# Making the low halves of the first feed-forward weights with an accumulating DMA instead of a VectorE subtraction

## The chip, the cores and the metric

The program runs on one core of one Trainium2 chip. The metric is the device time of one execution in microseconds, the median of several runs. The engines are named as the profile names them: PE is TensorE (PEld its weight loads), DVE is VectorE, ACT is ScalarE, POOL is GpSimd and SP is SyncE, which here only issues DMAs.

## What is computed

Two transformer layers on a sequence of 512 positions of width 1024, and a final norm. Each layer has a projection, two groups of attention heads and an output projection, and after that a feed-forward part with 4096 hidden units and a squared ReLU:

```python
        x = x + jnp.einsum('bse,ed->bsd', mixed, w_o[l])

        h = rmsnorm(x, mlp_norm[l])
        u = jnp.square(jax.nn.relu(jnp.einsum('bsd,df->bsf', h, w_ff1[l])))
        x = x + jnp.einsum('bsf,fd->bsd', u, w_ff2[l])
    return rmsnorm(x, final_norm)
```

All of it is float32. The change touches only how the weights `w_ff1` of the first quarter of the hidden units are made ready for PE.

## The kernel before

**Products in three parts.** PE multiplies operands of the type fp32r. To keep float32 accuracy, every operand is split into a high part, its value rounded to fp32r, and a low part, the rest that the rounding left. A product is then three matmuls (function `three`, L298 to L302): high by high (L300), high weight by low activation (L301), low weight by high activation (L302). So each weight tile `raw` of 128 x 1024 floats gets a pair `whi` and `wlo`: `whi` is a rounding copy on ACT (L117), `wlo` is `raw - whi`, a subtraction on DVE (L133).

**Units and their order.** The weights are cut into units of 128 x 1024 floats that are used in a fixed order (`_unit_list`). In each layer come the projections, then eight units of the output projection (kind "o"), then the feed-forward part in four groups. Group 0 has eight units of kind "1": unit ("1", l, f) holds the 1024 x 128 block of `w_ff1` for 128 hidden units. In the order they are the units 32 to 39 of layer 0 and 170 to 177 of layer 1, and the instruction order below shows them with these numbers (`raw32`, `whi32`, `wlo32`). The groups 1 to 3 work otherwise (seven combined forms per quarter) and are not touched. After the eight units of group 0 come the units of `w_ff2` (kind "f", tiles named `q`).

**One unit on PE.** `block` takes a unit and makes, for eight slices of 128 input dimensions, three matmuls each of 128 x 128 by 128 x 512, 24 in all, into one bank named `f`. The low part of the weights is needed by the third matmul of the block. After the block `evict_whole` on ACT and DVE makes ReLU, square and their splits.

**When a unit is split.** `next` is called when PE's work on unit i is written, and calls `do_split` for the units ahead: two ahead while there is one pool of split tiles (two pairs), four ahead once the feed-forward part has added a second pool (`W.pools.append(f2)`), as far as the pair that a unit takes belongs to no unit still to be used. So unit 32 is split while the output projection still runs, into the pair of unit 30; unit 33 takes the pair of unit 31; units 34 and 36 take the two pairs of the new pool; units 35 and 39 take the pair of unit 32, unit 38 that of unit 33 and unit 37 that of unit 34. A program that lays out the instructions then sets each engine's order by priorities; the order on each engine is fixed before the run.

**Loads.** `raw` tiles stand in a ring of three. SP loads them (L110); a load waits until the tile three units before it has been read. POOL issues the DMAs that add to what stands in a tile (`accum_op=ALU.add`), at L879, L886 and L911: they make sums of weight blocks for the later groups. POOL's instructions run in their written order, so a DMA there waits for the one ahead of it to be issued.

Of the kernel before, what the change touches and what calls it, by code (L numbers as in the profile page):

```python
# [12 lines left out]
AF = mybir.ActivationFunctionType  # L13
ALU = mybir.AluOpType
# [37 lines left out]
def _unit_list():  # L52
    units = []
    def qk(l, cq, ck, b):
        units.append(("p", l, cq + b * P))
        units.append(("p", l, ck + b * P))

    for l in range(L):
        for item in ORDER:
            b = int(item[1])  # L60
            if item[0] == "d":
                units.append(("x", l, b, 0))
                units.append(("x", l, b, 1))
            elif item[0] == "s":
                qk(l, SBQ, SBK, b)
            elif item[0] == "w":
                units.extend(("w", l, part) for part in range(4))
            else:
                units.extend(("v", l, SBV + b * P, half) for half in range(2))
        for half in (1, 0):  # L70
            for j in range(4):
                units.append(("o", l, half, j))
        for g in range(GROUPS):
            if g == 0:
                units.extend(("1", l, f) for f in range(2 * GP))
            else:
                units.extend(("s", l, g, j, form) for j in range(2) for form in FORMS)
            for form in FORMS2:
                for c in range(GP // 2):
                    units.append(("f", l, g, form, c))  # L80
    return units


_UNITS = _unit_list()
# [4 lines left out]
_SLOT = {u: n for n, u in enumerate(_RING)}  # L89
# [4 lines left out]
class _Weights:  # L94
# [24 lines left out]
    def split_part(self, i, a, b):  # L119
        nc = self.nc  # L120
        if i not in self.tiles and i in self.home:
            self.tiles[i] = self.home[i]
        if i not in self.tiles:
            k = self.spot(i)
            self.owner[k] = i
            self.turn = k + 1
            hi = self.pools[k // 2].tile([P, 1024], F32R, tag="whi", name=f"whi{i}")
            lo = self.pools[k // 2].tile([P, 1024], F32R, tag="wlo", name=f"wlo{i}")
            self.tiles[i] = (hi, lo)
        hi, lo = self.tiles[i]  # L130
        raw = self.first if (i, b) == (0, P) else self.raw[i]
        h = self.round(hi[:, a:b], raw[:, a:b])
        self.last = h, nc.vector.tensor_tensor(  # L133
            out=lo[:, a:b], in0=raw[:, a:b], in1=hi[:, a:b].bitcast(F32), op=ALU.subtract)

# [1244 lines left out]
```

## Time and profile before

| what | value |
|---|---|
| median of three runs | 1123.38 us (1123.38 to 1124.75) |
| the profiled execution, its own time | 1124.32 us |
| its span from the first to the last instruction | 1122.5 us |
| first feed-forward group in the span, layer 0 | 238.6 to 282.7 us |
| the same in layer 1 | 793.9 to 841.6 us |

The profile is of one execution. Its span lies 1.8 us below that execution's own time, and that execution is 0.94 us above the median of the three runs. Rows of a timeline give start, duration, engine, line, operation, output and inputs, and in brackets how long the engine was idle before and what released it. The tiles' numbers are left out there: `whi<-raw` is any unit's rounding. Since ACT's order is fixed, the eight roundings `whi<-raw` of a layer's group 0 are the last eight before the first `whi<-q`.

### The profile page before, as it was taken

The numbers are of one execution on the slowest core, as the hardware profiler recorded it, in microseconds if no ns is written. First come the engines' busy times: TensorE is split into PE (matmuls) and PEld (weight loads), VectorE is DVE, ScalarE is ACT, GpSimd is POOL, SyncE is SP. The second block draws the span as 40 slices with busy tenths as digits, with TensorE's granted clock in tenths as the row PEclk, the third lists the DMA queues.
The fourth block names the chain that finished last, engine by engine and source line by source line (L and its number), as shares of the span: only waits on it lengthen the run. The fifth ranks groups of instructions, "written<-read, shape, count | busy, mean of one in ns | idle before, by whom it ended". The sixth has DMA issues, their size and how long they took to land.

```text
span 1122.5 us, 17199 instructions
## 1 busy us (share of the span) xinstructions
PE 1114.8 (99%) x6377; PEld 977.4 (87%) x6377; DVE 903.5 (80%) x1309; ACT 683.3 (61%) x1107; POOL 154.3 (14%) x233
## 2 busy tenths in 40 slices
PE   9999999999999999999999999999999999999997
PEld 6889889888899899899878898988888998998986
DVE  7788788798668778779877887887787788797787
ACT  6446666667558458467344566665774584674665
POOL 1001343101011001001000014430010010010011
PEclk9999999999999999999999999999999999999999
DMA  7466343269688678658324654612577877687462
GB/s 243 143 190 186 110 131 117 69 222 230 173 214 182 175 200 186 189 132 210 110 75 146 198 146 131 166 60 76 206 174 185 205 177 185 183 187 206 114 132 94
DMA packets 61043, 181.25 MB, mean 161 GB/s; under 512 B 7456, under 2 KB 8736, under 8 KB 60960
## 3 DMA queue, kind: packets, MB, share of 16 engines
q1 hardware_dynamic: 50160, 141.84, 40.1%
q0 software_dynamic: 10368, 37.75, 19.1%
q8 instruction: 50, 0.82, 0.3%
q10 hardware_dynamic: 432, 0.56, 0.1%
q14 instruction: 33, 0.27, 0.1%
HBM read 150.77 MB, written 4.19 MB: 138 GB/s over the span
## 4 chain that ended last, share of the span: by engine, by line
PE 98%; DVE 1%; DMA 0%; ACT 0%; issue 0%; POOL 0%; SPq 0%; POOLq 0%; DVEq 0%
PE X L300 9%; PE X L302 9%; PE X L301 9%; PE V L300 4%; PE V L301 4%; PE V L302 4%; PE wo L300 3%; PE wo L302 3%; PE wo L301 3%; PE f L302 3%; PE f L300 3%; PE f L301 3%; PE Y L301 2%; PE Y L302 2%; PE Y L300 2%; PE W L302 1%
## 5 line engine op out<-in xcount | busy, mean ns | idle before, releaser
L117 ACT ACTIVATE whi<-q 128x1024 fp32r<-128x1024 f32 x96 | 101.6, 1059 | 108.5 <-PE X L302 38.1
L133 DVE TENSOR_TENSOR wlo<-q,whi 128x1024 fp32r<-128x1024 f32 x96 | 117.2, 1222 | 46.4 <-ACT whi L117 46.2
L133 DVE TENSOR_TENSOR wlo<-raw,whi 128x1024 fp32r<-128x1024 f32 (+1 forms) x82 | 97.2, 1192 | 11.1 <-ACT whi L117 11.0
L117 ACT ACTIVATE whi<-raw 128x1024 fp32r<-128x1024 f32 (+1 forms) x82 | 80.9, 993 | 38.3 <-issue 8.9
L300 PE MATMUL X<-whi,Ah 128*128 128x512 f32 x248 | 97.6, 393 | 0.0
L301 PE MATMUL X<-wlo,Ah 128*128 128x512 f32 x248 | 96.7, 390 | 0.0
L302 PE MATMUL X<-whi,Al 128*128 128x512 f32 x248 | 96.7, 390 | 0.0
L133 DVE TENSOR_TENSOR wlo<-waves,whi 128x1024 fp32r<-128x1024 f32 x40 | 48.9, 1222 | 16.5 <-ACT whi L117 16.4
L117 ACT ACTIVATE whi<-waves 128x1024 fp32r<-128x1024 f32 x40 | 42.2, 1055 | 29.7 <-PE X L302 20.5
L300 PEld LDWEIGHTS X<-whi,Ah 128*128 128x128 f32 x248 | 46.6, 188 | 12.0 <-DVE y L1104 1.9
L302 PEld LDWEIGHTS X<-whi,Al 128*128 128x128 f32 x248 | 46.5, 188 | 9.8
L301 PEld LDWEIGHTS X<-wlo,Ah 128*128 128x128 f32 x248 | 46.6, 188 | 9.0
L302 PE MATMUL X<-h_hi,wlo 128*128 128x256 f32 x192 | 54.3, 283 | 0.0
L300 PE MATMUL X<-hxh,whi 128*128 128x256 f32 x192 | 54.3, 283 | 0.0
L301 PE MATMUL X<-hxl,whi 128*128 128x256 f32 x192 | 54.3, 283 | 0.0
L302 PE MATMUL X<-hxh,wlo 128*128 128x256 f32 x192 | 54.3, 283 | 0.0
L301 PE MATMUL X<-h_lo,whi 128*128 128x256 f32 x192 | 54.3, 283 | 0.0
L300 PE MATMUL X<-h_hi,whi 128*128 128x256 f32 x192 | 54.3, 283 | 0.0
L300 PE MATMUL f<-h_hi,whi 128*128 128x512 f32 x128 | 50.4, 394 | 0.0
L302 PE MATMUL f<-h_hi,wlo 128*128 128x512 f32 x128 | 49.9, 390 | 0.0
L301 PE MATMUL f<-h_lo,whi 128*128 128x512 f32 x128 | 49.8, 389 | 0.0
L240 DVE TENSOR_TENSOR Al<-x,Ah 128x512 fp32r<-128x512 f32 (+1 forms) x60 | 46.6, 793 | 3.8 <-ACT Ah L239 3.5
(712 smaller groups left out, 3701.6 us busy)
## 6 DMA issues: line engine op xcount, KB each, us to landing
raw<-in_w SPq DMA_DIRECT2D x78, 512.0 KB, 3.6
q<-in_w SPq DMA_DIRECT2D x48, 512.0 KB, 4.5
q<-in_w POOLq DMA_DIRECT2D x48, 512.0 KB, 7.5
waves<-in_w SPq DMA_DIRECT2D x28, 512.0 KB, 4.4
first_a<-in_w SPq DMA_DIRECT2D x12, 512.0 KB, 4.9
first_b<-in_w SPq DMA_DIRECT2D x12, 512.0 KB, 5.1
first_c<-in_w SPq DMA_DIRECT2D x12, 512.0 KB, 4.2
first_b<-in_w POOLq DMA_DIRECT2D x12, 512.0 KB, 6.8
```

The lines of the kernel that those rows point to most:

```text
L117: return self.nc.scalar.activation(o, src, AF.Copy)
L133: self.last = h, nc.vector.tensor_tensor(out=lo[:, a:b], in0=raw[:, a:b], in1=hi[:, a:b].bitcast(F32), op=ALU.subtract)
L240: nc.vector.tensor_tensor(out=lo, in0=src, in1=hi.bitcast(F32), op=ALU.subtract)
L300: nc.tensor.matmul(pt, ah, bh, start=first, stop=False, skip_group_check=goes_on),
L301: nc.tensor.matmul(pt, ah, bl, start=False, stop=False, skip_group_check=goes_on),
L302: nc.tensor.matmul(pt, al, bh, start=False, stop=last, skip_group_check=goes_on))
```

## The change

For units of kind "1", `wlo` is no longer made by DVE. ACT first writes the negative rounding into `wlo` (a copy with the scale -1, new L134), and then POOL issues a DMA (new L135) that adds the weights themselves from DRAM onto it: `wlo = -round(raw) + raw`. All other units still go through the subtraction. Lines of the changed kernel behind this place are four higher than in the kernel before.

```diff
         hi, lo = self.tiles[i]
         raw = self.first if (i, b) == (0, P) else self.raw[i]
         h = self.round(hi[:, a:b], raw[:, a:b])
+        if _UNITS[i][0] == "1":
+            nc.scalar.activation(lo[:, a:b], raw[:, a:b], AF.Copy, scale=-1.0)
+            self.last = h, nc.gpsimd.dma_start(lo[:, a:b], self.dram[_SLOT[i]][:, a:b], accum_op=ALU.add)
+            return
         self.last = h, nc.vector.tensor_tensor(
             out=lo[:, a:b], in0=raw[:, a:b], in1=hi[:, a:b].bitcast(F32), op=ALU.subtract)
```

The order of ACT at the end of layer 0's output projection, before the change (`h_hi` and `sq` are the splits and squares of the residual stream after each of its output blocks, L1005 begins the combined forms for the later groups):

```order
L259 ACTIVATE sq_2649<-x_71 128x512
L117 ACTIVATE whi32_2671<-raw32_2587 128x1024
L250 ACTIVATE h_hi_72<-x_71,begin_70 128x512
L259 ACTIVATE sq_2668<-x_71 128x512
L250 ACTIVATE h_hi_72<-x_71,begin_70 128x512
L259 ACTIVATE sq_2693<-x_71 128x512
L117 ACTIVATE whi33_2755<-raw33_2631 128x1024
L250 ACTIVATE h_hi_72<-x_71,begin_70 128x512
L259 ACTIVATE sq_2712<-x_71 128x512
L1005 ACTIVATE x_71<-x_71,begin_70 128x256 x4
L117 ACTIVATE whi34_2761<-raw34_2675 128x1024
```

The same place in the changed kernel:

```order
L263 ACTIVATE sq_2649<-x_71 128x512
L117 ACTIVATE whi32_2671<-raw32_2587 128x1024
L134 ACTIVATE wlo32_2672<-raw32_2587 128x1024
L254 ACTIVATE h_hi_72<-x_71,begin_70 128x512
L263 ACTIVATE sq_2668<-x_71 128x512
L254 ACTIVATE h_hi_72<-x_71,begin_70 128x512
L263 ACTIVATE sq_2694<-x_71 128x512
L117 ACTIVATE whi33_2756<-raw33_2631 128x1024
L134 ACTIVATE wlo33_2757<-raw33_2631 128x1024
L254 ACTIVATE h_hi_72<-x_71,begin_70 128x512
L263 ACTIVATE sq_2713<-x_71 128x512
L1009 ACTIVATE x_71<-x_71,begin_70 128x256 x3
```

The roundings stand where they stood, and each negated copy stands right behind its rounding.

POOL's order at the start of group 0 of layer 0, before the change (the last attention product, then the accumulating DMAs for the groups behind):

```order
L567 TENSOR_TENSOR sig0s313_2439<-sig0s313_2439,C0s313_2440 128x512
L879 DMA q10_0_2734<-in_w2 128x1024
L879 DMA q11_0_2735<-in_w2 128x1024
L911 DMA first_b0_2910<-in_w1 128x1024
L886 DMA q00_0_2732<-in_w2 128x1024
```

And in the changed kernel:

```order
L571 TENSOR_TENSOR sig0s313_2439<-sig0s313_2439,C0s313_2440 128x512
L135 DMA wlo32_2672<-in_w 128x1024
L135 DMA wlo33_2757<-in_w 128x1024
L135 DMA wlo34_2764<-in_w 128x1024
L135 DMA wlo35_2851<-in_w 128x1024
L135 DMA wlo36_2858<-in_w 128x1024
L883 DMA q10_0_2735<-in_w2 128x1024
L883 DMA q11_0_2736<-in_w2 128x1024
L135 DMA wlo37_2904<-in_w 128x1024
L135 DMA wlo38_2913<-in_w 128x1024
L915 DMA first_b0_2917<-in_w1 128x1024
L135 DMA wlo39_2968<-in_w 128x1024
```

Five of the eight new DMAs stand ahead of `q10` and `q11`, two behind them, and the last behind `first_b0`.

ACT's order further on in the changed kernel, at the third block's eviction (`norms<-f` is that eviction, the `Ah` rows are splits of the activations):

```order
L117 ACTIVATE whi38_2912<-raw38_2862 128x1024
L978 ACTIVATE norms_74<-f0_0_2_2849 128x512
L117 ACTIVATE whi37_2903<-raw37_2855 128x1024
L248 ACTIVATE Ah0_0_2738<-waves_75 128x256
L243 ACTIVATE Ah0_0_2738<-waves_75 128x256
L979 ACTIVATE norms_74<-norms_74 128x512
L134 ACTIVATE wlo37_2904<-raw37_2855 128x1024
L243 ACTIVATE Ah0_0_2738<-norms_74 128x256
L134 ACTIVATE wlo38_2913<-raw38_2862 128x1024
```

Here the negated copies do not follow their roundings directly: three small rows stand between those of unit 37.

## The prediction

> **What bounds the kernel now.** I read the page's first and fourth part first: who is busy, and which engine the chain that ended last runs over.
>
> ```profile
> PE 1114.8 (99%) x6377; PEld 977.4 (87%) x6377; DVE 903.5 (80%) x1309; ACT 683.3 (61%) x1107; POOL 154.3 (14%) x233
> PE 98%; DVE 1%; DMA 0%; ACT 0%; issue 0%; POOL 0%; SPq 0%; POOLq 0%; DVEq 0%
> ```
>
> PE is busy for 99% of the span and holds 98% of the chain. So nothing that DVE gives up can shorten the program unless PE waits for DVE somewhere, and everything that makes PE wait lengthens it by that wait. The PE column of the table of windows shows whether PE waits in the stage of the change (its columns: window and length, busy time of PE, PEld, DVE, ACT and POOL, granted clock, DMA share, GB/s).
>
> ```profile
> 238.00:244.00 6.00, 6.00 (x28) 4.99 (x27) 5.21 (x9) 5.17 (x10) 0.00 (x0) 1.00 0.53 181
> 244.00:250.00 6.00, 6.00 (x30) 4.94 (x29) 6.00 (x12) 4.13 (x6) 0.00 (x0) 1.00 0.91 321
> 794.00:800.00 6.00, 6.00 (x28) 4.99 (x27) 4.35 (x6) 4.25 (x6) 0.00 (x0) 1.00 0.32 103
> 800.00:806.00 6.00, 6.00 (x32) 4.95 (x32) 4.98 (x8) 3.80 (x7) 0.00 (x0) 1.00 0.91 309
> 244.00:262.00 18.00, 18.00 (x83) 14.89 (x82) 18.00 (x36) 13.26 (x20) 1.98 (x2) 1.00 0.89 304
> ```
>
> PE is busy without a gap at the start of group 0 in both layers. DVE is full from 244 to 262 us, and PE does not feel it. The list of PEld's waits by releaser, for the whole span, begins with this row (total, times, longest):
>
> ```profile
> PEld X L300 <- DVE y L1104: 1.9, 5, 0.4
> ```
>
> The longest entry that names DVE is 1.9 us, and it belongs to the chains `X`, behind group 0's blocks. So the most that a lighter DVE could give in this program is of that size, and in the stage of the change it is zero.
>
> **What goes and what comes.** The page's groups price the two instructions:
>
> ```profile
> L117 ACT ACTIVATE whi<-raw 128x1024 fp32r<-128x1024 f32 (+1 forms) x82 | 80.9, 993 | 38.3 <-issue 8.9
> L133 DVE TENSOR_TENSOR wlo<-raw,whi 128x1024 fp32r<-128x1024 f32 (+1 forms) x82 | 97.2, 1192 | 11.1 <-ACT whi L117 11.0
> ```
>
> The mean over both shapes is 1.19 us for the subtraction; the full shape takes 1.22 us below. Sixteen units (eight in each layer) lose it: 16 x 1.22 = 19.5 us of DVE work, worth nothing on the path. The same units gain a copy of ACT's price, 16 x 1.05 = 17 us by the rows below; ACT is busy 13.3 of 18 us in the fullest window, so most of the eight copies of a layer find room. They count only where they stand between a rounding and its DMA. And sixteen accumulating DMAs of 512 KB come on POOL's queue. Their latency is the whole matter: 1.2 us of DVE is replaced by a copy, a hand-over to POOL and a DMA.
>
> **The first block's wait.** The timeline gives when unit 32 (and its counterpart in layer 1) is rounded, and when PE asks for its low half, the third weight load of the block:
>
> ```profile
> 233.68 1.05 ACT L117 ACTIVATE whi<-raw 128x1024 fp32r<-128x1024 f32 x1
> 235.16 1.22 DVE L133 TENSOR_TENSOR wlo<-raw,whi 128x1024 fp32r<-128x1024 f32 x1
> 239.10 0.19 PEld L302 LDWEIGHTS f<-h_hi,wlo 128*128 128x128 f32 x1
> 789.26 1.04 ACT L117 ACTIVATE whi<-raw 128x1024 fp32r<-128x1024 f32 x1
> 794.40 0.19 PEld L302 LDWEIGHTS f<-h_hi,wlo 128*128 128x128 f32 x1
> ```
>
> Now DVE is done at 235.16 + 1.22 = 236.38, 2.72 us ahead of need. The rounding cannot start earlier after the change: it waits for the pair of unit 30, and stands behind the same `sq` row in ACT's order. From its start to PE's need there are 5.42 us in layer 0 and 5.14 us in layer 1. In that time the new chain has to fit:
>
> ```profile
> 799.04 2.01 ACT L117 ACTIVATE whi<-raw 128x1024 fp32r<-128x1024 f32 x2 [1.21 <-issue]
> 267.86 1.23 DVE L133 TENSOR_TENSOR wlo<-q,whi 128x1024 fp32r<-128x1024 f32 x1
> 269.38 0.87 POOL L886 DMA_DIRECT2D q<-in_w x1 [1.85 <-DVE wlo L133]
> ```
>
> Two copies of this size in a row end 2.01 us after the first began. POOL starts a DMA 269.38 - 269.09 = 0.29 us after the instruction it waits for. So the DMA is issued 2.30 us after the rounding's start, and 3.12 us (layer 0) or 2.84 us (layer 1) are left for it to land.
>
> An accumulating DMA of 512 KB into SBUF is what L879, L886 and L911 issue 72 times. The views by line give issue to landing, minimum, median and maximum; here for L911, then for L886, then for the two of L879 at 257 us, in the fullest stretch:
>
> ```profile
> L911 POOL DMA_DIRECT2D norms<-in_w x12: 860/875/898, 294.2 to 1039.5; - x12
> ...
> DMA to landing us min/median/max: 5.4/6.3/7.9
> L886 POOL DMA_DIRECT2D q<-in_w x32: 856/875/1147, 269.4 to 1081.2; - x32
> ...
> DMA to landing us min/median/max: 5.3/7.5/9.8
> DMA to landing us min/median/max: 8.0/9.0/10.1
> ```
>
> None landed in under 5.3 us. Near 236 us the DMA share is about a half (0.53 in the window above) and in layer 1 a third, yet one load of 512 KB shares the engines with the new DMA: the load into the ring that the same copy releases. I take **6.6 us**, near L911's median, and keep 5.3 and 8.0 as ends (the short one for a free queue, the long one for the fullest stretch). PE's wait is then 6.6 - 3.12 = **3.5 us** in layer 0 (2.2 to 4.9) and 6.6 - 2.84 = **3.8 us** in layer 1 (2.5 to 5.2). PE runs in order, so nothing fills it.
>
> **The second block.** Unit 33 is rounded when unit 31 is done with its pair, before the wait, so its DMA does not move with it:
>
> ```profile
> 239.42 1.04 ACT L117 ACTIVATE whi<-raw 128x1024 fp32r<-128x1024 f32 x1
> 244.54 0.19 PEld L302 LDWEIGHTS f<-h_hi,wlo 128*128 128x128 f32 x1
> 795.00 1.04 ACT L117 ACTIVATE whi<-raw 128x1024 fp32r<-128x1024 f32 x1
> 799.84 0.19 PEld L302 LDWEIGHTS f<-h_hi,wlo 128*128 128x128 f32 x1
> ```
>
> It has 5.12 us, and the first wait adds its length. The second wait is 2.30 + latency - 5.12 - (first latency - 3.12) = 0.30 us plus what the second DMA takes longer than the first. In layer 1 it has 4.84 us, and again 0.30 remains. The stretch that it falls in is fuller (0.91 after 244 and after 800 us), and the copy ahead of it shifts ACT by a tenth; I take **0.6 us** in each layer (0 to 2).
>
> **The later blocks.** Unit 34 is rounded at 243.77 and needed here:
>
> ```profile
> 243.77 1.04 ACT L117 ACTIVATE whi<-raw 128x1024 fp32r<-128x1024 f32 x1
> 250.47 0.19 PEld L302 LDWEIGHTS f<-h_hi,wlo 128*128 128x128 f32 x1
> 256.46 1.05 ACT L117 ACTIVATE whi<-raw 128x1024 fp32r<-128x1024 f32 x1
> 257.71 0.62 ACT L975 ACTIVATE norms<-norms 128x512 f32<-128x512 f32 x1
> 266.79 0.19 PEld L302 LDWEIGHTS f<-h_hi,wlo 128*128 128x128 f32 x1
> ```
>
> It has 6.70 us plus the waits so far, 4.1: its DMA may take 8.5 us, and I count nothing. Unit 37 (the row at 256.46 and the last) is the worst placed. Its rounding waits until PE has finished the third block, so earlier waits don't help it; it has 10.33 us. In ACT's new order three small rows stand before its negated copy (L975 and two of 256 columns, which I put at 0.4 each), some 1.5 us, and on POOL its DMA stands behind `q10` and `q11`. Copy done after 3.6 us, issue at 3.9, so the DMA may take 6.4 us. I count **0.5 us** in layer 0 (0 to 3). In layer 1 the blocks are longer by transposes (L1113) and I count nothing. Units 35, 36, 38 and 39 have two blocks or more, and I count nothing for them either.
>
> **The sum.** 3.5 + 3.8 + 0.6 + 0.6 + 0.5 = 9.0 us. On the profiled execution's own 1124.32 us that is 1133.3; that execution is 0.94 us above the median of 1123.38, which would give 1132.4. I put 1133.
>
> **The rivals.** *The queue backs up* (20%). An accumulating DMA holds the sixteen engines for long: the page's third part gives
>
> ```profile
> q0 software_dynamic: 10368, 37.75, 19.1%
> ```
>
> for 72 DMAs, so 0.191 x 1122.5 / 72 = 2.98 us each. From 244 to 262 us the engines are already taken 0.89 of the time, 16 us, and five new DMAs bring 15 us more. If they push one another, units 35 and 37 come late too, some 3 us more in layer 0 and 2 in layer 1: about 1138. Against it: most of what is loaded there is for later groups and can wait.
>
> *The clock drops in the wait* (12%). After PE's last matmul the windows show
>
> ```profile
> 1116.60:1121.50 4.90, 0.00 (x0) 0.00 (x0) 1.65 (x4) 1.90 (x4) 0.54 (x1) 1.00 0.70 263
> 1121.80:1122.50 0.70, 0.00 (x0) 0.00 (x0) 0.00 (x0) 0.00 (x0) 0.00 (x0) 0.50 0.00 0
> 1.36 3.60 PE L223 MATMUL warm<-edge 128*128 128x512 bf16 x8 [1.36 <-POOL edge L217]
> ```
>
> so full clock over 4.9 idle microseconds, half of it later. The last row is the start: eight matmuls of 512 columns take 3.60 us, 0.45 each, against 0.227 in the block (24 from 239.10 to 244.54). A wait that drops the clock would cost about half of 3.6 us, 1.8 us more, twice at most: 1135 to 1137. My waits of 3.5 and 3.8 us are shorter than the 4.9 seen without a drop, and that speaks against it. The Trainium skill, in "TensorE: Matmul & The Clock Gate", section "Part 1: The HAM clock gate", says that the clock halves after at least one idle window of about 3.4 us, and that the windows run free; by that rule a wait of 3.5 us drops it only when it happens to cover a window, and the trace's end agrees.
>
> *Quick DMAs* (10%): all land in 5.3 us, nothing else is late: 2.2 + 2.5 = 4.7 us, about 1128.
>
> *Not slower* (3%). If the new DMA landed within 3.1 us of its issue, PE would find the low half of unit 32 in place in both layers and the time would stay at 1124 give or take a microsecond. The point that decides is 3.12 and 2.84 us from issue to landing; the row of 5.3 as the minimum speaks against it. The Trainium skill gives such a price: "DMA: Bandwidth & Descriptors", section "Anatomy of one DMA", fits a DMA from GpSimd with 2.0 us plus bytes by 436 GB/s, which for 512 KB is an estimate of 3.2 us. By it the waits would be 0.1 and 0.4 us and the time 1125. The trace does not agree for DMAs that accumulate.
>
> **How the numbers follow.** The forecast, 1130 to 1137, has 55%. The range reaches from the quick DMAs to the backed-up queue with long first waits (4.9 + 5.2 + 2 + 2 + 3 = 17): 1128 to 1140. A measurement of this kernel can tell about 0.2%, 2.2 us, from no change. Slower by more than that is everything but the last rival: 0.96; within it 0.03; faster 0.01, since no wait of PE in the stage goes away.
>
> **What would show it.** In the changed kernel PEld's waits should have a row for `f` at L302, released by the DMA `wlo<-in_w`: about 4 us after the second load of the first block in each layer, and a small one in the second block. ACT's negated copies should take 1.05 us, the new DMAs 5.3 to 8 us. DVE should be less busy by 19 us with no effect. The prediction is wrong if PE stays without a gap there, if a third or later block waits for more than 2 us, or if the granted clock falls under 1.00 behind a wait.

## The result and the profile after

The changed kernel takes 1148.62 us in the median of four runs against 1123.65 us for the kernel before on the same chip. One of the four took 1378.73 us at a mean granted clock of 0.75; the ratio of 1.0215 [1.0201, 1.0229] (in brackets the 95% interval) leaves it out, and the median of the other three is 1147.29 us. Run four times more, the same kernel takes 1148.75 us against 1123.72 us, 25.0 us slower, and the profile read here is of that run (1148.21 us in the profiled execution, span 1146.4 us). The forecast was 1133 us with a range up to 1140. The direction was right and the size was not: the change costs nearly three times the 9 us that the sum gave.

The page's first and third part, for this kernel:

```profile
PE 1124.2 (98%) x6377; PEld 983.3 (86%) x6377; DVE 886.6 (77%) x1293; ACT 697.0 (61%) x1123; POOL 167.6 (15%) x249
q0 software_dynamic: 12672, 46.14, 22.4%
```

DVE gave up 903.5 - 886.6 = 16.9 us, ACT took on 13.7, and POOL issues 16 more transfers. PE's own busy time grew by 9.4 us although it has the same 6377 matmuls; most of that is its clock, below. The list of waits by releaser now has a row that was not there before (total, times, longest):

```profile
PEld f L306 <- DMA wlo<-in_w: 16.8, 5, 6.3
```

The timeline of the weight loads shows the five. The number in brackets is the wait.

```profile
241.83 0.29 PEld L306 LDWEIGHTS f<-h_hi,wlo 128*128 128x128 f32 x1 [3.53 <-DMA wlo<-in_w]
...
261.89 0.18 PEld L306 LDWEIGHTS f<-h_hi,wlo 128*128 128x128 f32 x1 [0.76 <-DMA wlo<-in_w]
...
278.93 0.29 PEld L306 LDWEIGHTS f<-h_hi,wlo 128*128 128x128 f32 x1 [6.29 <-DMA wlo<-in_w]
...
812.59 0.19 PEld L306 LDWEIGHTS f<-h_hi,wlo 128*128 128x128 f32 x1 [3.41 <-DMA wlo<-in_w]
...
848.23 0.28 PEld L306 LDWEIGHTS f<-h_hi,wlo 128*128 128x128 f32 x1 [2.87 <-DMA wlo<-in_w]
```

In layer 0 the first, fourth and sixth block wait, in layer 1 the first and the sixth. The two first blocks wait 3.53 and 3.41 us, as the sum had it. The sixth blocks (unit 37 and its counterpart) wait 6.29 and 2.87 us, where it had 0.5 and 0. The durations of the third loads themselves (0.29 and 0.28 instead of 0.19) already point to the second loss, which the table of windows states in its column of the granted clock (after the busy times; then DMA share and GB/s):

```profile
242.00:248.00 6.00, 6.00 (x15) 4.67 (x16) 3.07 (x8) 2.91 (x5) 0.87 (x1) 0.54 0.95 220
...
268.00:276.00 8.00, 5.07 (x23) 3.87 (x21) 4.89 (x10) 6.46 (x11) 5.12 (x6) 1.00 1.06 305
...
279.00:285.00 6.00, 6.00 (x14) 4.72 (x15) 0.00 (x0) 0.00 (x0) 0.00 (x0) 0.50 1.07 210
```

Behind the first wait PE runs at a clock of 0.54, behind the sixth block's at 0.50: 14 matmuls in 6 us, where the kernel before had 28 in the window quoted in the prediction. The records of the clock put it at a half from 240.70 to 247.53, 278.25 to 285.07, 814.14 to 817.55 and 848.27 to 851.68 us: once in or just behind each wait over 2.8 us. What that costs is read from the third load of such a block to the first load of the next. Undisturbed it is 244.09 - 239.10 = 4.99 us in the kernel before; here are the ends for the four blocks, first the row of before, then those of after:

```profile
244.09 0.19 PEld L300 LDWEIGHTS f<-h_hi,whi 128*128 128x128 f32 x1
```

```profile
249.37 0.19 PEld L304 LDWEIGHTS f<-h_hi,whi 128*128 128x128 f32 x1
...
286.67 0.19 PEld L304 LDWEIGHTS f<-h_hi,whi 128*128 128x128 f32 x1
...
819.10 0.19 PEld L304 LDWEIGHTS f<-h_hi,whi 128*128 128x128 f32 x1
...
854.71 0.19 PEld L304 LDWEIGHTS f<-h_hi,whi 128*128 128x128 f32 x1
```

249.37 - 241.83 = 7.54, then 7.74, 6.51 and 6.48 us: 2.55 + 2.75 + 1.52 + 1.49 = 8.3 us over the undisturbed length. Waits and half clock together are 16.8 + 8.3 = 25.1 us, and 25.0 were measured. The two profiles can also be laid side by side, weight load by weight load, since both have the same 6377: the changed kernel falls 15.6 us behind in layer 0's group and 9.2 us in layer 1's, 24.8 in all. Elsewhere it gains 0.8 us in the first 10 us of the program and keeps its distance to a tenth. So the account closes to within half a microsecond; what remains is why the sixth blocks wait, and what the clock is worth by itself.

For the first question, here are ACT's rounding and negated copy of unit 37, then POOL's DMAs (`q10`, `q11`, and units 37 and 38 in one row), then SP's row with the load for `q11` (the first of its two), and at last the row with that load in the kernel before:

```profile
261.64 1.05 ACT L117 ACTIVATE whi<-raw 128x1024 fp32r<-128x1024 f32 x1
263.72 1.05 ACT L134 ACTIVATE wlo<-raw 128x1024 fp32r<-128x1024 f32 x1
```

```profile
256.61 0.86 POOL L883 DMA_DIRECT2D q<-in_w  x1
268.19 0.86 POOL L883 DMA_DIRECT2D q<-in_w  x1 [10.72 <-DMA q<-in_w]
268.78 2.08 POOL L135 DMA_DIRECT2D wlo<-in_w  x2
```

```profile
255.80 1.18 SPq L881 DMA_DIRECT2D q<-in_w  x2
```

```profile
249.52 2.17 SPq L877 DMA_DIRECT2D q<-in_w  x3
```

Unit 37's copy is done at 264.77, and its DMA starts at 268.78. POOL has stood for 10.72 us, until 268.19, before `q11`, whose tile is still being loaded. That load was issued by SP at 255.80 and landed at 267.90; in the kernel before its like was issued near 250. Once issued, unit 37's DMA takes 278.89 - 268.78 = 10.11 us, in a stretch whose DMA share is 1.06 (0.80 before).

### The profile page after: what moved, and what is told of

The parts are those of the page before. It is cut to its first block, busy times and chain, and to the rows that moved or that the text cites. A ratio compares the mean times of both kernels' runs of the same rounds, so it can differ in the third digit from the quotient of the medians.

```text
span 1377.0 us, 17230 instructions
## 1 busy us (share of the span) xinstructions
PE 1364.3 (99%) x6377; PEld 1087.2 (79%) x6377; DVE 899.2 (65%) x1293; ACT 704.3 (51%) x1123; POOL 158.8 (12%) x249
## 4 chain that ended last, share of the span: by engine, by line
PE 74%; DMA 2%; issue 2%; ACT 0%; DVE 0%; POOL 0%; POOLq 0%; DVEq 0%; SPq 0%
PE X L306 9%; PE X L305 9%; PE X L304 9%; PE V L304 4%; PE V L305 4%; PE V L306 4%; PE Y L304 2%; PE Y L306 2%; PE Y L305 2%; PE f L306 2%; PE f L305 2%; PE f L304 2%; DMA wlo<-in_w 1%; PE W L305 1%; PE W L306 1%
## 5 line engine op out<-in xcount | busy, mean ns | idle before, releaser
L304 PE MATMUL X<-whi,Ah 128*128 128x512 f32 x248 | 113.4, 457 | 0.0
L305 PE MATMUL X<-wlo,Ah 128*128 128x512 f32 x248 | 112.9, 455 | 0.0
L306 PE MATMUL X<-whi,Al 128*128 128x512 f32 x248 | 112.9, 455 | 0.0
L137 DVE TENSOR_TENSOR wlo<-raw,whi 128x1024 fp32r<-128x1024 f32 (+1 forms) x66 | 76.2, 1160 | 13.9 <-ACT whi L117 12.1
L117 ACT ACTIVATE whi<-waves 128x1024 fp32r<-128x1024 f32 x40 | 42.4, 1060 | 53.9 <-PE X L306 38.3
L306 PE MATMUL f<-h_hi,wlo 128*128 128x512 f32 x128 | 60.0, 469 | 5.2 <-DMA wlo<-in_w 5.2
L306 PE MATMUL X<-h_hi,wlo 128*128 128x256 f32 x192 | 60.9, 317 | 0.0
L304 PE MATMUL X<-h_hi,whi 128*128 128x256 f32 x192 | 60.8, 316 | 0.0
L305 PE MATMUL X<-h_lo,whi 128*128 128x256 f32 x192 | 60.7, 316 | 0.0
L304 PE MATMUL f<-h_hi,whi 128*128 128x512 f32 x128 | 59.3, 463 | 0.0
L305 PE MATMUL f<-h_lo,whi 128*128 128x512 f32 x128 | 58.5, 457 | 0.0
L244 DVE TENSOR_TENSOR Al<-x,Ah 128x512 fp32r<-128x512 f32 (+1 forms) x60 | 47.7, 794 | 12.1 <-ACT Ah L243 10.6
```

The lines of the kernel that those rows point to most:

```text
L117: return self.nc.scalar.activation(o, src, AF.Copy)
L137: self.last = h, nc.vector.tensor_tensor(out=lo[:, a:b], in0=raw[:, a:b], in1=hi[:, a:b].bitcast(F32), op=ALU.subtract)
L244: nc.vector.tensor_tensor(out=lo, in0=src, in1=hi.bitcast(F32), op=ALU.subtract)
L304: nc.tensor.matmul(pt, ah, bh, start=first, stop=False, skip_group_check=goes_on),
L305: nc.tensor.matmul(pt, ah, bl, start=False, stop=False, skip_group_check=goes_on),
L306: nc.tensor.matmul(pt, al, bh, start=False, stop=last, skip_group_check=goes_on))
```

## The experiments

Three theories were put to the test, and the recorded expectations go by these letters. A: PE waits for the landing of the new DMAs, and each long wait halves its clock for a while. B: the longer way through ACT (two copies in a row) is what costs. C: the later blocks wait because of their DMAs' place on POOL's queue. Blocks are counted from 0 in the edits (`_UNITS[i][2]`). Beside each result stands the ratio to the kernel before on the same chip, with its 95% interval.

**The changed kernel again**, no edit.

> The changed kernel once more, for a profile at full clock. Theory A (late landing, then a lowered clock): near 1147 us; PE waits at the third matmul of the first block in both layers by 3.3 to 3.8 us, the granted clock falls to 0.5 behind some of these waits, and the later blocks wait too because the transfers that add to a tile take 8 to 13 us where several are under way. Sum of PE's waits some 15 us, and some 8 us more from the clock. Theory B (ACT is held up by the added copies): PE would wait for evictions or splits on ACT, not for transfers.

Measured: 1148.75 us, 1.0223 [1.0207, 1.0238]. This is the run read above.

**Only the first two blocks changed**, and **only the last six**:

```diff
-        if _UNITS[i][0] == "1":
+        if _UNITS[i][0] == "1" and _UNITS[i][2] < 2:
```

> Only the first two units of the group are made the new way, the other six as before. If the two first blocks' waits and the clock behind them are the loss: 1135 to 1140 us, half of the loss or more. If the queue of added transfers is the loss: about 1131 to 1133 us, the two first waits of 3.5 to 3.8 us alone.

> Only the units three to eight of the group are made the new way. If the loss comes from the first two blocks: within 2 us of before. If the transfers back up behind one another: 1130 to 1138 us, with waits of PE for the low halves of the third to the sixth block in layer 0, less in layer 1, where the blocks are longer.

Measured: 1135.77 us, 1.0107 [1.0090, 1.0124], and 1142.46 us, 1.0166 [1.0149, 1.0183]. The first two blocks alone cost 12.1 us: waits of 3.70 and 4.14 us and a half clock behind both. The last six cost 18.7 us with no wait in the first block at all; PEld's row there is

```profile
PEld f L306 <- DMA wlo<-in_w: 15.6, 5, 6.2
```

That is more than the 1138 us that the expectation gave at most. The longest stands at the third block of layer 0 (6.18 us), which in the full change does not wait, since the waits ahead give it time. So the parts don't add (12.1 + 18.7 is more than 25.0): a wait early in the group is lead for the blocks behind it. The later blocks are the larger part, not the small rest that the prediction made of them.

**The copies without the DMA.** ACT's negated copy stays, DVE adds the weights to it:

```diff
-            self.last = h, nc.gpsimd.dma_start(lo[:, a:b], self.dram[_SLOT[i]][:, a:b], accum_op=ALU.add)
+            self.last = h, nc.vector.tensor_tensor(
+                out=lo[:, a:b], in0=raw[:, a:b], in1=lo[:, a:b].bitcast(F32), op=ALU.add)
```

> The negated copy is added on ACT for all eight units, but DVE makes the sum and no transfer is added: the low half is the negated rounding plus the weights. Theory A: within 1.5 us of before, since 17 us of ACT work beside PE cost nothing. Theory B: at least 8 us slower than before.

Measured: 1124.0 us, 1.0001 [0.9992, 1.0011]. Sixteen copies on ACT and their place ahead of the low half cost nothing that can be told. Theory B falls; all 25 us come with the DMAs.

**Plain DMAs.** The same DMAs without the addition. The subtraction is left out here: the low halves hold the whole weights.

```diff
-            self.last = h, nc.gpsimd.dma_start(lo[:, a:b], self.dram[_SLOT[i]][:, a:b], accum_op=ALU.add)
+            self.last = h, nc.gpsimd.dma_start(lo[:, a:b], self.dram[_SLOT[i]][:, a:b])
```

> As the changed kernel, but the eight transfers overwrite the low half with the weights instead of adding to it (the subtraction is left out, so the low halves hold the whole weights). Theory A1 (what is long about the transfer is the adding): issue to landing near 4 us instead of 6.4 to 13, first waits near 1 us, the time 1125 to 1130 us. Theory A2 (what is long is the path over POOL and the shared engines, adding or not): first waits still 3 us or more and the time above 1140 us.

Measured: 1134.1 us, 1.0093 [1.0078, 1.0108]. The view of L135 and PEld's row:

```profile
DMA to landing us min/median/max: 4.4/7.5/10.7
```

```profile
PEld f L306 <- DMA wlo<-in_w: 9.4, 7, 2.5
```

The same view of the changed kernel has 6.4/9.7/13.0. The addition makes a DMA some 2 us later, and 25.0 us of loss become 10.3: 7.4 less by shorter waits (9.4 instead of 16.8), and the rest because the clock was halved behind only one of them (2.46 us), for 3.41 us. The time lies between the two theories, with first waits of 1.61 and 1.37 us: adding makes up more than half of the loss, but a plain DMA from POOL doesn't meet its time here either.

**Unit 38's DMA ahead of `q10` and `q11`.** In the function that fetches the sums, these two are put behind the DMA of block 6 in the order:

```diff
-                    nc.gpsimd.dma_start(t, quad(g, "22", c), accum_op=ALU.add)
+                    d = nc.gpsimd.dma_start(t, quad(g, "22", c), accum_op=ALU.add)
+                    if g == 0:
+                        behind(d, W.rest_of[_INDEX[("1", l, 6)]])
```

> As the changed kernel, but on POOL the transfers of q10 and q11 are put behind those of the units six and seven of the group. Theory C (the sixth block's wait of 6.3 us in layer 0 comes from standing behind q11 on POOL, whose own load landed late): that wait falls under 2 us, the one of layer 1 under 1 us, the clock stays up there, and the time is 1134 to 1139 us. Theory D (the engines are full and the order does not matter): the waits stay within 2 us of what they were and the time stays above 1144 us.

Measured: 1147.16 us, 1.0205 [1.0188, 1.0222], as slow as the change. Units 37 and 38 are now issued ahead of `q10` and `q11`, and the sixth blocks no longer wait. But the eighth does:

```profile
263.13 0.19 PEld L306 LDWEIGHTS f<-h_hi,wlo 128*128 128x128 f32 x1 [0.95 <-DMA wlo<-in_w]
...
288.19 0.25 PEld L306 LDWEIGHTS f<-h_hi,wlo 128*128 128x128 f32 x1 [3.41 <-DMA wlo<-in_w]
```

Unit 39's DMA still stood behind the others. The sum of the waits is 16.8 us again, in 5, but not for the order alone: the later blocks wait 7.4 us instead of 9.9, and the first blocks 9.5 instead of 6.9, because their DMAs took 8.22 and 7.24 us this time, for a reason that no run shows. The order decides which block waits (C), and moving two sums a few places mostly passes the wait on.

**All eight DMAs first.** The group's DMAs go in the units' order, ahead of `first_b`, `q10` and `q11`; two fetches are written a block later for that, and the negated copies are chained.

```diff
+            if _UNITS[i][2]:
+                self.behind(h, self.low[0])
+                self.behind(d, self.low[1])
+            self.low = m, d
...
+                    if g == 0:
+                        for f in (5, 6, 7):
+                            behind(d, W.rest_of[_INDEX[("1", l, f)]])
...
-            for k, role in ((5, "a"), (6, "b"), (7, "c")):
+            for k, role in ((5, "a"), (7, "b"), (7, "c")):
...
-                        for form, at in (("x3", 3), ("21", 5)):
+                        for form, at in (("x3", 4), ("21", 5)):
```

> As the changed kernel, but on POOL all eight transfers of the group stand ahead of q10, q11 and first_b, in the order of the units. If the later blocks' waits come from the order on POOL's queue, where transfers are served one after the other: only the first blocks wait (3.5 to 5 us in each layer, and up to 1.5 us at the fourth block), clock low twice, 1133 to 1139 us. If the queue is too full in any order: waits appear at other blocks, 16 us in sum, and over 1143 us.

Measured: 1137.12 us, 1.0116 [1.0099, 1.0133]. POOL's row for units 37 and 38, and PEld's waits:

```profile
264.35 1.76 POOL L135 DMA_DIRECT2D wlo<-in_w  x2 [8.68 <-ACT wlo L134]
```

```profile
PEld f L311 <- DMA wlo<-in_w: 10.3, 5, 3.7
```

The DMA of unit 37 now goes out when its copy is done (264.35 instead of 268.78), and no block behind the fourth waits. That gives back 1148.75 - 1137.12 = 11.6 of the 25 us. How much of it is the order is not shown: the loads that were put off may leave the engines freer as well, and unit 37's DMA took 8.08 us instead of 10.11. What remains are the two first waits (3.73 and 3.63 us), 1.77 us at the fourth block, and two small ones.

**Only the blocks with the longest lead** (5th, 7th and 8th):

```diff
+        if _UNITS[i][0] == "1" and _UNITS[i][2] in (4, 6, 7):
```

> Only units 36, 38 and 39 (and their counterparts in layer 1) are made the new way, those that have two blocks or more between the end of their negated copy and PE's need. If lead time decides: within 2 us of before (1123 to 1126 us), no wait of PE for a transfer over 1 us, clock 1.00. If an added transfer costs by itself (engines shared with the loads): over 1128 us.

Measured: 1125.6 us (ten runs, 1123.65 to 1131.14), 1.0018 [1.0004, 1.0031]. In the profiled execution (1123.65 us) all that is left is

```profile
PEld f L306 <- DMA wlo<-in_w: 0.3, 1, 0.3
```

while the six DMAs took 7.5 to 10.8 us. So these DMAs are as slow as the others; what makes them cheap is that PE asks later than they land. The executions above 1128 us have a mean granted clock of 0.996 to 0.998 instead of 1.000, which fits a wait with half clock behind it; but only one execution was profiled, and that the DMAs were later in the others is not shown.

**The price of the clock.** First the first block alone, then the same with 16 matmuls on zeros, not part of the reference's work, between the second and third matmul of that block, so that PE is kept busy while it waits:

```diff
+        if _UNITS[i][0] == "1" and _UNITS[i][2] == 0:
...
+                for _ in range(16):
+                    d = nc.tensor.matmul(fill, zeros[:, 0:128], zeros[:, 128:640], start=True, stop=True)
```

> Only the first unit of the group (32, and 170 in layer 1) is made the new way. The wait before the first block stays, 3.5 to 4 us in each layer, and nothing later waits for a transfer. If the lowered clock costs on top of the wait: block by block 1.5 to 2.5 us more, 1133 to 1136 us. If it costs nothing: 1131 to 1132 us.

> The same with 16 matmuls on zeros, 3.4 us, in the place of the first block's wait. If the clock costs: granted clock 1.00, 2 to 4 us faster than the kernel before it in this call. If not: equal to it, or slower by what the added matmuls take beyond the wait.

Measured: 1137.09 us, 1.0119 [1.0104, 1.0134], and 1134.1 us, 1.0094 [1.0077, 1.0110]. The waits in the profile, each with the first load of the next block, first unfilled, then filled (the unfilled waits are longer than was expected, and so is the time):

```profile
244.54 0.29 PEld L306 LDWEIGHTS f<-h_hi,wlo 128*128 128x128 f32 x1 [5.16 <-DMA wlo<-in_w]
...
251.48 0.19 PEld L304 LDWEIGHTS f<-h_hi,whi 128*128 128x128 f32 x1
...
806.99 0.29 PEld L306 LDWEIGHTS f<-h_hi,wlo 128*128 128x128 f32 x1 [5.21 <-DMA wlo<-in_w]
...
814.28 0.19 PEld L304 LDWEIGHTS f<-h_hi,whi 128*128 128x128 f32 x1
```

```profile
243.65 0.19 PEld L327 LDWEIGHTS f<-h_hi,wlo 128*128 128x128 f32 x1 [1.87 <-DMA wlo<-in_w]
...
248.56 0.19 PEld L304 LDWEIGHTS f<-h_hi,whi 128*128 128x128 f32 x1
...
804.02 0.19 PEld L327 LDWEIGHTS f<-h_hi,wlo 128*128 128x128 f32 x1 [1.67 <-DMA wlo<-in_w]
...
808.95 0.19 PEld L304 LDWEIGHTS f<-h_hi,whi 128*128 128x128 f32 x1
```

And the windows behind the wait, in the same order:

```profile
245.00:249.00 4.00, 4.00 (x11) 3.07 (x11) 2.11 (x3) 0.14 (x1) 0.00 (x0) 0.51 0.97 321
```

```profile
245.00:249.00 4.00, 4.00 (x19) 3.29 (x18) 3.96 (x7) 1.31 (x2) 0.00 (x0) 1.00 0.90 274
```

The DMAs land 8.2 us (unfilled) and 8.3 and 8.0 us (filled) after their issue, so PE goes on at about the same point in the filled kernel; only it goes on at full clock, 19 matmuls in 4 us instead of 11. From the first load of the block to the third it takes 5.58 and 5.62 us unfilled, 5.68 and 5.48 filled; from there to the next block 6.94 and 7.29 us unfilled, 4.91 and 4.93 filled. So the half clock is worth 2.0 and 2.4 us in these two executions, and 1137.09 - 1134.1 = 3.0 us for two waits, 1.5 us each, in the medians (the unfilled execution profiled is the slowest of its four, 1139.18 us). The clock is a cause by itself.

**Three fillings that say less.** The same filling on the first two blocks, on the change in the order of unit 38 first, and on the change with all units first.

> As the kernel with only the first two units made the new way (1135.8 us), with 16 matmuls on zeros put between the second and the third matmul of the first block, 3.4 us of PE work in the place of the wait. If the lowered clock behind the first waits is part of the loss: the granted clock stays 1.00 there, and the time falls to 1130 to 1132 us though PE does more. If it is the wait alone: 1135 to 1137 us, or more by what the added matmuls take.

> All eight units the new way, with both edits: q10 and q11 behind on POOL, and 16 matmuls on zeros in the first block. If waits, queue order and clock are the whole loss: about 1131 to 1133 us, the two first waits of 3.5 us each and up to 2 us of others, clock 1.00 throughout. If something else is lost too: above 1136 us.

> As the kernel before it in this call, with 16 matmuls on zeros in the place of the first block's wait. If the clock behind the first waits is a loss of its own: 2 to 4 us faster than without them and clock 1.00 throughout. If the slow stretch lies where PE would wait for the second block's low half anyway: within 1.5 us of it, with a wait of 1 to 2 us at the second block instead.

Measured: 1134.85 us, 1.0098 [1.0083, 1.0113]; 1161.19 us, 1.0338 [1.0321, 1.0355]; 1148.25 us, 1.0213 [1.0198, 1.0229]. In the first the clock stays at 1.00 in the group and still only 0.9 us are won against the first two blocks unfilled: the second block, reached sooner, waits for its own DMA, which it doesn't otherwise (third load at 249.59, 1.83 us of wait). The other two were to be faster than without the filling and came out slower, by 14.0 and 11.1 us. The added matmuls changed the orders that the program lays out for all engines, and unit 37's DMA went out late again: in the last one at

```profile
271.33 1.75 POOL L135 DMA_DIRECT2D wlo<-in_w  x2 [15.64 <-ACT wlo L134]
```

instead of 264.35, and the sixth block of layer 0 waited 4.95 us. This time POOL stood for ACT: unit 37's negated copy was done at 271.04 instead of 264.06. These two change two things at once and tell nothing of the clock by itself; they do show again what a late issue of that DMA costs. No version was faster than the kernel before.

## Where the prediction held and where it failed

**What bounds the kernel** held. DVE is lighter by 16.9 us (19 were forecast) and nothing is faster; the copies cost nothing (1.0001 with them alone). The direction, and that the latency of the new DMAs is the whole matter, held as well.

**The first block's wait** held: 3.5 and 3.8 us forecast, 3.53 and 3.41 measured, with DMAs of 6.54 and 6.40 us where 6.6 was taken. That is partly luck: with the first block alone the same DMA took 8.2 us and PE waited 5.2 us, just outside the upper ends. **The second block** was given 0.6 us and waits for no DMA, because the first block, on half clock, gave it 2.55 us more in layer 0 and 1.52 in layer 1; in the kernel with the first two blocks changed and the first filled, where the clock stays up, it waits 1.83 and 0.71 us.

**The later blocks** are the step that failed. The prediction counted 0.5 us for unit 37, by "Copy done after 3.6 us, issue at 3.9, so the DMA may take 6.4 us." The copy was done 264.77 - 261.64 = 3.1 us after the rounding's start (the start is read from ACT's timeline). The issue came after 268.78 - 261.64 = 7.1 us, not 3.9, because POOL stood before `q11`; and the DMA took 10.1 us, not 6.4. From the rounding to the landing that makes 17.2 us, and PE's need came after (278.93 - 6.29) - 261.64 = 11.0: the wait of 6.3 us. The later issue makes 3.2 us of it and the longer DMA 3.7, less 0.7 because PE asked later than forecast. The prediction's own list of POOL's order showed `q10` and `q11` ahead of unit 37, but asked only what is queued, not when `q11`'s tile would be loaded. That load moved with the change: SP's loads of `raw` stand ahead of it, they wait for negated copies (the load at 253.53 follows a copy that ends at 253.50), and the copies wait for pairs that PE holds longer by the first wait and the half clock. In all the later blocks were worth 6.29 + 0.76 + 2.87 = 9.9 us of wait instead of 0.5. The lengths stood in the prediction too: its row for the fullest stretch has 8.0 to 10.1 us, and its rival of the backed-up queue counts 16 us of the engines taken and 15 us new in a stretch of 18; unit 37 was still given no more than 6.4.

**The clock** is the second failure: nothing was counted, with 12% for a drop, 1.8 us each and twice at most. It came four times and cost 8.3 us. The argument against it, "My waits of 3.5 and 3.8 us are shorter than the 4.9 seen without a drop", took one idle stretch at the program's end for a threshold. In the profiles of the experiments, every wait of 3.69 us or more had half clock in it or just behind it (14 of 14), of the nine between 2.8 and 3.63 us six had, and one of 2.46 us too. The low time came as 3.41, 6.83 or 10.24 us. The Trainium skill, "TensorE: Matmul & The Clock Gate", section "Part 1: The HAM clock gate", says that the clock halves after at least one idle window of about 3.4 us, and that the windows run free. The low times in multiples of 3.41 us agree with such a window, and so does it that waits of like length came out differently. That a whole window must be idle does not agree with the runs: half clock followed waits of 2.46, 2.87, 3.02 and 3.07 us, and in the run read above it set in at 240.70, 2.4 us after the first wait had begun. The prediction took the rule as a reason to expect a drop only now and then; the runs say that a wait of 3.4 to 3.8 us loses the clock more often than not. The price was near: 8.3 us for four is 2.1 each.

**The rivals.** "The queue backs up" and "The clock drops in the wait" both came true, each larger in all than priced, and the range took them as alternatives. They are not: a queue that backs up makes waits long enough to drop the clock. The range's top had 17 us of waits, close to the 16.8 measured, and no clock. "Quick DMAs" and "Not slower" fell. The estimate of 3.2 us by the Trainium skill, "DMA: Bandwidth & Descriptors", section "Anatomy of one DMA", was too short for either kind: the quickest plain DMA of 512 KB from POOL took 4.4 us here, the quickest adding one of L135 6.4 us.

**Left open:** the first adding DMA of a layer took between 6.4 and 8.4 us in the kernels here that make the first block the new way (6.38 in layer 0 and 8.14 in layer 1 of one of them), and no run tells why. That the late load of `q11`, and not only its place, makes the sixth block late was read from the trace and not tried by itself.

## What to carry to other kernels

Where a step of an engine is replaced by a DMA, compare the lead (from the last operand ready to the first use) with the latency seen in that stage, for every unit apart, and follow what each queue ahead of it waits for after the change; the average of a quiet stage doesn't hold in a full one. On a kernel that PE bounds, price each wait of about 3 us or more with the half clock behind it, and treat "the wait is longer" and "the clock drops" as one case. An engine at 80% with nothing waiting for it is no reason to move its work.

## What the runs showed of the hardware

- A wait of PE of 3.4 to 3.8 us was followed by half clock in six cases of seven; the price by itself was 1.5 us per wait in the medians (for waits of 5.2 us), and 16 matmuls on zeros in the wait kept the clock at 1.00.
- Adding in the DMA takes the DMA engines longer than copying. By the profile's third part the 72 adding DMAs of the kernel before take 2.98 us of 16 engines each. If those take the same in the other kernels, the 16 of L135 add 0.224 x 1146.4 - 214.4 = 42.4 us, 2.7 each; as plain DMAs they add 0.212 x 1132.5 - 214.4 = 25.7 us, 1.6 each.
- Queued adding DMAs of 512 KB landed 2.5 us apart (unit 37 at 278.89, unit 38 at 281.38, `first_b` at 283.86, unit 39 at 286.34, by the landings of layer 0 in the run read above), close to the 2.7 that one takes of the engines: each one ahead in the queue costs about its own length.
- An edit that only adds matmuls moved a DMA by 7 us on POOL (264.35 against 271.33) by way of the copy on ACT that it waits for, in kernels 11 us apart: an experiment in such a program is read only after looking at the orders.
